# Full-row score products, late head norms and a different order of fill in a two-layer hybrid encoder

## The chip, the cores and the metric

The kernel runs on one core of a Trainium2 chip. Its time is the device time of one execution in microseconds (us). A core has a matrix engine (TensorE, PE in the profile; its weight loads are shown apart as PEld), a vector engine (VectorE, DVE), an activation engine (ScalarE, ACT), a general engine (GpSimd, POOL) and a queue engine that issues transfers (SyncE, SP). They run side by side and wait for each other through semaphores. Matrix results land in PSUM, which has eight banks of 512 fp32 columns here: four buffers called `mm`, two called `sc` (scores) and two called `tr` (transposes). All else lies in SBUF.

## The reference, cut to what matters

Batch 1, 512 tokens in a grid of 8 x 64, width 1024, two layers, fp32. Each layer does three things to x:

```python
h = rms_norm(x, norm_mix)
proj = h @ w_in                          # local q,k,v (8 heads x 64), then g_q (8), g_k (2), g_v (2)
na  = neighbourhood_attention(...)       # 8 heads, window 8 x 16, learned bias
g_q = rope(rms_norm(g_q per head, q_norm)); g_k = rope(rms_norm(g_k per head, k_norm))
gqa = softmax(g_q @ g_k.T * 64**-0.5) @ g_v       # 8 query heads over 2 key heads
x = x + concat([na, gqa]) @ w_out
q = rms_norm(x, norm_mem_q) @ w_mem_q             # 4 heads x 128
k, v = rms_norm(mem, norm_mem_kv) @ w_mem_kv      # 256 memory tokens
x = x + softmax(q @ k.T * 128**-0.5) @ v @ w_mem_o
u = conv3(rms_norm(x, norm_ffn) @ w_up) ; x = x + (silu(gate) * val) @ w_down
```

A last RMS norm follows.

## The kernel before, in words

x is held transposed, features on partitions, as eight tiles `xT` of 128 x 512. Every operand of a product is split in two: a high part in the fp32r format, made by an ACT copy, and a low part, the rest, made by a subtraction. A product is then three matmuls (`mm3`): high by high, high by low, low by high. Weights come as `raw` tiles over SP's queue, and `emit_split` (L192, L193) casts them on ACT and subtracts on POOL or DVE; the order of all weights is written out in `plan_layer`, and `get_w` hands them out in that order, splitting a few ahead.

PE and SP keep the program's order. ACT, DVE and POOL instructions are put in order by a scheduler when the program is built.

The order on PE is woven by hand. `weave` runs pipeline steps of attention units (scores, normalise, transpose, values), each a fixed number of rounds behind the other, and between them takes steps of a `Filler`, a list of generators with projection work. `NA_FILL`, `GQA_FILL` and `MEM_FILL` say how many steps of fill each round gets; `MEM_STEPS` does so for the statistics and operands of the memory in layer 0.

A layer runs through these stages. First comes local attention (`na_...`), eight units of two heads and two query blocks, with the projections of q, k, v and then of the grouped heads (`gqa_project`) as fill. `split_qk` scales a projected q or k, and makes the stacked operand: for q one tile per head with the high part in the head's 64 partitions and the low part in the other 64; for k the high part in both halves, and the low part apart. The scores of one head are therefore a 128-row matmul (q high and low by k high) and a 64-row one (q high by k low). `na_normalise` scales the exponentials by the reciprocal sums, half of them on DVE and half on POOL (`normalise`, L388).

`gqa_rope` norms and rotates the heads of one block of 128 tokens: ACT copies them out of PSUM (L684) and squares them (L686), DVE sums, multiplies by the cosine table (L690), POOL multiplies by the sine table (L695), and an inverse root is taken (L312 on DVE, L314 on POOL). One block later, through `late` and `tick`, `gqa_rope_end` adds the two products (L701) and multiplies by the root (L702).

Then four rounds of `gqa_transpose` turn the heads and build the same kind of stacked operands (L719 to L728), and sixteen units of grouped-query attention follow, with fill: memory keys, memory values, the output product of the local heads (`out_na`), and the first rows of the output product of the grouped heads (`close_rows("outg", ...)`). `fold` brings the two heads of a pair, which lie in one half of the partitions, into one tile.

`close_rows` finishes a row of x: it keeps three rows open until the last operand is there, and `Norm.close` adds x (L339), makes the next norm's operand (ACT L348, DVE L349), copies x back (ACT L341) and squares it (ACT L353, sums on POOL L364). Memory attention then projects its queries from the unnormed operand; the norm's factor, `rs`, enters as scale of the exponentials (L911, L915), so the scores need not wait for the statistics. The FFN comes last.

## Time and profile before

| what | before |
|---|---|
| time, median of 3 (lowest to highest) | 1415.34 us (1415.29 to 1416.22) |
| the profiled execution's own time | 1416.86 us |
| its span | 1415.0 us |
| mean granted clock of TensorE | 0.992 |
| matmuls | 7236 |
| transfers | 128.61 MB, mean 91 GB/s |

The span is the time between the first and the last instruction that the profiler saw; the remaining 1.86 us lie around it. Rows of the profile name an engine, a line of the kernel, the operation, the tile written and the tiles read. Almost all PE work has line L60, a helper, so it is told apart by the tiles: `mm<-xg,hi` is a projection with a normed x, `sc` are scores, `tr` transposes. Matmuls overlap in the records: the time of one from start to end is longer than the distance to the next one's start, and this distance is what it costs.

### The profile page before, as it was taken

How to read it: one execution, taken by the hardware profiler on the slowest of the kernel's cores; microseconds unless marked ns; L12 is line 12 of the kernel's file. 1: busy time of each engine (PE TensorE's matmuls, PEld its weight loads, DVE VectorE, ACT ScalarE, POOL GpSimd, SP SyncE). 2: the span in 40 equal slices, each digit the busy share in tenths (PEclk: the TensorE clock that was granted, in tenths of full speed). 3: DMA queues.
4: the chain of work that ended last, by engine and by line, in shares of the span. 5: the costliest groups of instructions: out<-in, count | busy, mean ns of one | idle time of the engine just before them, and what ended most of it. 6: DMA issues, size and time to landing. Idle time of an engine off the chain costs nothing.

```text
span 1415.0 us, 19554 instructions
## 1 busy us (share of the span) xinstructions
PE 1366.4 (97%) x7236; PEld 1152.7 (81%) x7236; DVE 932.9 (66%) x1606; ACT 720.3 (51%) x1350; POOL 700.5 (50%) x509
## 2 busy tenths in 40 slices
PE   8999799989999999999999998999899999999997
PEld 7788777877888888888888887788788888888897
DVE  5889977565588169458457898754738843871874
ACT  5776667656443234233557666766555432432441
POOL 2347755734444444544544686456164444444452
PEclk9999999999999999999999999999999999999999
DMA  6431321222333333332343223122133333333331
GB/s 211 152 97 46 91 75 31 76 74 60 90 104 90 104 110 106 97 104 84 96 147 99 83 62 118 31 61 89 31 91 101 91 105 90 101 91 106 88 91 60
DMA packets 207070, 128.61 MB, mean 91 GB/s; under 512 B 4608, under 2 KB 203520, under 8 KB 206976
## 3 DMA queue, kind: packets, MB, share of 16 engines
q1 hardware_dynamic: 206976, 127.37, 30.4%
q8 instruction: 57, 0.93, 0.3%
q14 instruction: 37, 0.30, 0.1%
HBM read 125.26 MB, written 2.10 MB: 90 GB/s over the span
## 4 chain that ended last, share of the span: by engine, by line
PE 77%; DVE 13%; ACT 5%; issue 2%; DMA 2%; POOL 1%; SPq 0%; DVEq 0%; ACTq 0%
PE mm L60 71%; PE tr L60 3%; PE sc L60 3%; DVE r L382 1%; ACT hi L192 1%; DVE t L645 1%; DMA raw<-in_w_in 1%; ACT t L603 1%; DVE t L388 1%; DVE r L548 1%; DVE sc L597 1%; DVE xg L721 1%; POOL lo L193 1%; DVE r L701 1%; DVE s L911 1%
## 5 line engine op out<-in xcount | busy, mean ns | idle before, releaser
L193 POOL TENSOR_TENSOR lo<-raw,hi 128x512 fp32r<-128x512 f32 (+2 forms) x264 | 501.1, 1909 | 522.9 <-ACT hi L192 520.8
L60 PE MATMUL mm<-xg,hi 128*128 128x512 f32 x1792 | 557.1, 392 | 4.4 <-DVE r L385 2.5
L60 PEld LDWEIGHTS mm<-xg,hi 128*128 128x128 f32 x1792 | 335.2, 189 | 74.6 <-issue 2.6
L192 ACT CAST hi<-raw 128x512 fp32r<-128x512 f32 (+2 forms) x276 | 224.5, 837 | 313.0 <-PE mm L60 257.8
L60 PE MATMUL mm<-xg,lo 128*128 128x512 f32 x896 | 350.1, 391 | 0.0
L60 PE MATMUL mm<-r,hi 128*128 128x512 f32 (+1 forms) x1160 | 338.7, 376 | 3.9 <-DVE r L385 2.3
L60 PEld LDWEIGHTS mm<-r,hi 128*128 128x128 f32 x1160 | 210.9, 190 | 43.0 <-issue 3.9
L1010 DVE SCALAR_TENSOR_TENSOR t<-t,par,t 128x7 f32<-128x7 f32 (+1 forms) x352 | 201.4, 639 | 32.0 <-ACT t L1003 31.6
L60 PE MATMUL mm<-r,lo 128*128 128x512 f32 (+1 forms) x580 | 216.8, 374 | 0.0
L60 PEld LDWEIGHTS mm<-xg,lo 128*128 128x128 f32 x896 | 168.7, 188 | 35.9 <-DVE lo L193 0.7
L60 PE MATMUL mm<-hi,xg 128*128 128x256 f32 x640 | 122.5, 286 | 4.1 <-ACT t L684 2.9
L60 PEld LDWEIGHTS mm<-r,lo 128*128 128x128 f32 x580 | 110.0, 190 | 19.3
L388 POOL TENSOR_SCALAR t<-t,s 128x512 f32<-128x512 f32 (+1 forms) x96 | 62.8, 667 | 111.7 <-DVE s L609 53.0
L995 DVE TENSOR_TENSOR t<-mm,rep 128x512 f32<-128x512 f32 x88 | 60.1, 687 | 75.5 <-PE mm L60 59.7
L60 PEld LDWEIGHTS mm<-hi,xg 128*128 128x128 f32 x640 | 101.9, 191 | 7.3 <-ACT t L684 3.9
L60 PE MATMUL mm<-r,r 128*128 128x256 f32 (+1 forms) x684 | 102.8, 299 | 3.8 <-DVE r L382 3.8
L60 PEld LDWEIGHTS mm<-r,r 128*128 128x128 f32 x684 | 88.7, 191 | 13.8 <-issue 5.9
L1012 ACT ACTIVATE t<-t 128x512 f32<-128x512 f32 x44 | 27.8, 633 | 127.1 <-DVE t L1010 127.1
L1039 DVE TENSOR_TENSOR xT<-xT,mm 128x512 f32<-128x512 f32 x32 | 22.0, 686 | 106.7 <-PE mm L60 106.7
L1016 DVE TENSOR_TENSOR r<-t,r 128x512 fp32r<-128x512 f32 x44 | 87.1, 1979 | 7.3 <-ACT r L1015 4.1
L60 PE MATMUL mm<-lo,xg 128*128 128x256 f32 x320 | 90.5, 283 | 0.0
L382 DVE TENSOR_TENSOR r<-tr,r 128x512 fp32r<-128x512 f32 x112 | 74.6, 685 | 6.8 <-ACT r L381 5.9
(129 smaller groups left out, 1652.5 us busy)
## 6 DMA issues: line engine op xcount, KB each, us to landing
raw<-in_w_up SPq DMA_DIRECT2D x88, 512.0 KB, 3.9
raw<-in_w_in SPq DMA_DIRECT2D x34, 512.0 KB, 4.1
raw<-in_w_down SPq DMA_DIRECT2D x32, 448.0 KB, 3.8
raw<-in_w_mem_kv SPq DMA_DIRECT2D x16, 512.0 KB, 3.8
raw<-in_w_down SPq DMA_DIRECT2D x16, 512.0 KB, 4.2
r<-in_bias SPq DMA_DIRECT2D x16, 384.0 KB, 4.7
raw<-in_w_out SPq DMA_DIRECT2D x8, 512.0 KB, 3.5
raw<-in_w_out SPq DMA_DIRECT2D x16, 256.0 KB, 4.2
```

The costliest lines, as they stand in the source:

```text
L60: return lambda *a, **k: self.tc.keep_in_program_order(op(*a, **k))
L192: act.copy(hi[:, k], raw[:, k])
L193: (POOL if eng[0] == "P" else DVE).tensor_sub(lo[:, k], raw[:, k], f(hi)[:, k])
L382: DVE.tensor_sub(lo, ps, f(hi))
L388: eng.tensor_scalar(e, e, sums[:, col : col + 1], 1.0, op0=ALU.mult, op1=ALU.mult)
L548: DVE.tensor_sub(v[o] if n == "q" else qk[n, p][2][r], u[r], f(v[r]))
L597: DVE.tensor_tensor_reduce(out=sc[j][:, i, :], in0=sc[j][:, i, :], in1=bias[p][j][:, WTYPE[b], :], op0=ALU.add, op1=ALU.min, scale=-1.0, s ...
L995: DVE.tensor_mul(u, us[side], ffn.rep)
L1010: DVE.scalar_tensor_tensor(cc[:, dst], u[:, src], wi, cc[:, dst], op0=ALU.mult, op1=ALU.add)
L1012: ACT.activation(cs[0], cs[0], AF.Silu)
L1016: DVE.tensor_sub(acts[j][1], cs[0], f(acts[j][0]))
L1039: DVE.tensor_add(xT[m], xT[m], pm)
```

## The change

The change has these parts, in both layers:

- Scores of both attentions: the low part of k is now stored in both halves of the partitions, so that the second score product is a full 128-row one as well. The number of matmuls stays.
- `split_qk` scales q and k in place in PSUM and splits from there; k's second copy is made on ACT.
- Local attention's weights: the half that DVE scaled is scaled on ACT.
- The grouped heads are projected in the order keys and values, first queries, second queries. The sums of squares of all blocks are gathered, and the inverse root is taken once per group. Rotated heads are added at once, from a product left in PSUM and POOL's product. k is multiplied by its root on POOL; q's root is the scale of the exponentials, with the bias multiplied by it on ACT.
- Memory keys are projected between the grouped heads' projections; memory values follow; half of the grouped heads' output product (two of four head pairs) is added to x in a generator of its own, and `close_rows` takes the other half. `outg` weights are cut in 2 x 512 columns instead of 4 x 256.
- `fold` writes each half of 256 columns directly as high and low parts.
- Memory queries are scaled by the norm's factor before they are split: the factor is spread over columns (`mq.spread()`), and the scores' maximum is used as it is.

The core of the diff:

```diff
+GQA_ORDER = [2, 0, 1]
+MEMK_AFTER = [(0,), (1, 2), (3,)]
-NA_FILL = [(2, 0, 0), (3, 0, 1), (2, 1, 1), (0, 1, 1), (1, 1, 1), (0, 2, 1), (1, 1, 1), (1, 1, 1), (1, 1, 1), (0, 3, 1)]
+NA_FILL = [(2, 0, 1), (2, 0, 1), (1, 1, 1), (1, 1, 1), (1, 1, 1), (1, 1, 1), (1, 1, 1), (1, 1, 1), (1, 1, 2), (1, 2, 1)]
-GQA_FILL = [1, 2, 1, 2, 1, 1, 1, 1, 1, 1, 1, 1, 1, 1, 1, 1, 1, 1, 0, 6]
+GQA_FILL = [1, 1, 1, 1, 1, 2, 1, 1, 1, 1, 2, 1, 1, 1, 1, 1, 1, 1, 0, 6]
-MEM_STEPS = [1, 0, 0, 1, 0, 2, 1, 0, 0, 3]
+MEM_STEPS = [1, 0, 1, 1, 1, 1, 2, 3, 0, 0]
...
     def split_qk(n, p, pm):
-            u = tmp()
             if n == "q":
-                DVE.scalar_tensor_tensor(u, pm, HD**-0.5, mix.rep, op0=ALU.mult, op1=ALU.mult)
+                DVE.scalar_tensor_tensor(pm, pm, HD**-0.5, mix.rep, op0=ALU.mult, op1=ALU.mult)
...
+            lows = rtile((2, S))
+            qk[n, p] += [lows[:, j] for j in range(2)]
+            for j, (v, r, o) in enumerate(halves):
+                for half in (r, o):
+                    DVE.tensor_sub(lows[half, j], pm[r], f(v[r]))
+                ACT.copy(v[o], pm[r])
...
                 for j in range(2):
-                    PE.matmul(sc[j][:, i, :], qst[j][:, qs], kst[j][:, ks], start=True, stop=False)
-                for j in range(2):
-                    r = slice(64 * j, 64 * j + 64)
-                    PE.matmul(sc[j][:, i, :], qst[j][r, qs], kst[2][r, ks], start=False, stop=True)
+                    for part in range(2):
+                        PE.matmul(sc[j][:, i, :], qst[j][:, qs], kst[2 * part + j][:, ks], start=part == 0, stop=part == 1)
...
-                    normalise(es[j][:, i, :], sums, 2 * j + i, POOL if i else DVE)
+                    if i:
+                        normalise(es[j][:, i, :], sums, 2 * j + i, POOL)
+                    else:
+                        ACT.activation(es[j][:, i, :], es[j][:, i, :], AF.Copy, scale=sums[:, 2 * j + i : 2 * j + i + 1])
...
+            ACT.activation(x, pv, AF.Copy, scale=r)
+            ACT.activation(tq, pv, AF.Square, scale=r)
+            DVE.scalar_tensor_tensor(pv, pv, r, gtab[0][:, 2 * qk, b, :].unsqueeze(1).to_broadcast([P, nh, HD]),
+                                     op0=ALU.mult, op1=ALU.mult)
+            DVE.tensor_reduce(hs, tq, axis=AX.X, op=ALU.add)
...
-            hr = rsqrt(hs, nh, 1.0 / HD)
-            late.append(lambda: gqa_rope_end(t1, t2[:, :nh], hr, nh))
-        def gqa_rope_end(t1, t2, hr, nh):
-            DVE.tensor_add(t1, t1, t2)
-            DVE.tensor_mul(t1, t1, hr.unsqueeze(2).to_broadcast([P, nh, HD]))
+            DVE.tensor_add(roped[b][:, g:8:2, :] if g < 2 else roped[b][:, 8:10, :], pv, t2)
...
-                        DVE.tensor_sub(gq[0][r, 5, bs], tr[r, 0], f(g[r, 4, bs]))
-                    for g, r, o in halves:
-                        DVE.tensor_copy(g[o, 4, bs], g[r, 4, bs])
+                        for half in (r, o):
+                            DVE.tensor_sub(g[half, 5, bs], tr[r, 0], f(g[r, 4, bs]))
+                        ACT.copy(g[o, 4, bs], tr[r, 0])
...
+                c, r = slice(j, j + 1), hq[j][:, 4 * b + i : 4 * b + i + 1]
+                DVE.tensor_reduce(nmx[:, c], sc[j], axis=AX.X, op=ALU.max, negate=True)
+                ACT.activation(nb[:, c], nmx[:, c], AF.Copy, scale=r)
-                ACT.activation(e, sc[j], AF.Exp, bias=nmx[:, j : j + 1], accum_out=sums[:, j : j + 1])
+                ACT.activation(e, sc[j], AF.Exp, bias=nb[:, c], scale=r, accum_out=sums[:, c])
...
+        def out_gqa():
+            for m in range(KC):
+                if m % 4 == 0:
+                    w = get_w(("outg", 0, m // 4))
+                pm = ps_mm()
+                gemm_T(pm, w, parts[4:6], range(2), 0, 1, slice(P * (m % 4), P * (m % 4) + P))
+                DVE.tensor_add(xT[m], xT[m], pm)
+                yield
...
-        fill = Filler(*([project_first(), *units[3:]] if l == 0 else units), gqa_project())
+        gqa = [gen for g, heads in zip(GQA_ORDER, MEMK_AFTER) for gen in (gqa_project(g), memory_keys(heads))]
+        fill = Filler(*([project_first(), *units[3:]] if l == 0 else units), *gqa)
...
-        fill = Filler(memory_keys(), memory_values(0), out_na(), memory_values(1), close_rows("outg", PartsView(parts, 4), nn))
+        fill = Filler(memory_values(0), memory_values(1), out_na(), out_gqa(), close_rows("outg", 1, PartsView(parts, 6), 2, nn))
...
+        def mem_query(h, pm):
+            DVE.scalar_tensor_tensor(pm, pm, 128.0**-0.5, mq.rep, op0=ALU.mult, op1=ALU.mult)
+            mqs[h] = rpair()
+            split_psum(*mqs[h], pm)
...
-            nmx, sums, nb = small(2), small(2), small(2)
+            nmx, sums = small(2), small(2)
             DVE.tensor_reduce(nmx, sc, axis=AX.X, op=ALU.max, negate=True)
-            DVE.tensor_mul(nb, nmx, rs[:, 2 * bp : 2 * bp + 2])
...
         mq.stat()
         fill.step(2)
-        DVE.tensor_scalar_mul(rs, mq.rstd, 128.0**-0.5)
+        mq.spread()
+        for h, pm in unscaled:
+            mem_query(h, pm)
+        unscaled = None
+        fill.step(1)
```

More of the change, by code (lines that the diff above doesn't have):

```diff
@@ L396, in fold @@
         for j, r in enumerate(rows):
-            DVE.tensor_add(o32[r, cs], po[0:64, j], th[r, j])
+            DVE.tensor_add(o32[r], po[0:64, j], th[r, j])
+        ACT.copy(out[0][:, cs], o32)
+        POOL.tensor_sub(out[1][:, cs], o32, f(out[0][:, cs]))
     def split_out(o32):
@@ L541, in split_qk @@
             for v, r, o in halves:
[L542 to L544 removed]
+                ACT.copy(v[r], pm[r])
+            if n == "q":
                 for v, r, o in halves:
[L546 to L548 removed]
+                    DVE.tensor_sub(v[o], pm[r], f(v[r]))
+                return
+            lows = rtile((2, S))
[4 more added lines that the diff above has]
+                ACT.copy(v[o], pm[r])
         vblk = [None, None]
@@ L680, in gqa_rope @@
+        def gqa_rope(g, b, pm, hs):
             nh = 4 if g < 2 else 2
```

166 lines of the change are left out of this document (78 added, 88 removed).

## The prediction

> **What bounds the kernel now.** I read the page's busy shares, then the windows of busy time by stage, then the groups of instructions inside the first attention stage, then the timeline around the edited places.
>
> ```profile
> PE 1366.4 (97%) x7236; PEld 1152.7 (81%) x7236; DVE 932.9 (66%) x1606; ACT 720.3 (51%) x1350; POOL 700.5 (50%) x509
> ...
> 50.00:180.00 130.00, 116.28 (x813) 104.52 (x813) 114.77 (x254) 89.62 (x216) 83.41 (x90) 0.99 0.28 86
> 180.00:265.00 85.00, 84.41 (x514) 68.05 (x515) 56.91 (x110) 58.24 (x135) 47.38 (x53) 1.00 0.21 57
> 265.00:292.00 27.00, 26.64 (x122) 21.91 (x121) 11.71 (x18) 17.94 (x30) 17.15 (x10) 1.00 0.26 78
> 292.00:330.00 38.00, 33.74 (x174) 27.35 (x174) 27.37 (x57) 20.20 (x51) 10.51 (x5) 0.96 0.18 56
> 740.00:870.00 130.00, 121.95 (x866) 110.95 (x864) 109.74 (x252) 89.06 (x213) 82.81 (x89) 0.99 0.31 95
> 981.00:1020.00 39.00, 34.73 (x181) 28.39 (x182) 27.38 (x57) 20.80 (x51) 10.52 (x5) 0.96 0.18 54
> 400.00:425.00 25.00, 25.00 (x112) 20.71 (x111) 21.44 (x30) 11.40 (x15) 10.74 (x5) 1.00 0.35 101
> ```
>
> The first column after the stretch is its length, then busy time of PE, PEld, DVE, ACT, POOL. PE is busy 97% of the span, so time comes from two places only: what PE is kept busy with, and about 48 us of holes (1415.0 less 1366.4). The holes lie where the change works. Local attention with its projections (50 to 180, and 740 to 870 in layer 1) leaves PE idle 13.7 and 8.05 us, and there DVE is the fullest of the others, at 88% and 84%. Memory attention (292 to 330, 981 to 1020) leaves 4.26 and 4.27 us. The grouped-query stage between (180 to 265) has no hole: 84.41 of 85. In the FFN a 512-column matmul takes a slot of 25.00/112 = 0.223 us.
>
> **Score products on all rows.** What a 64-row product costs is read from when the next instruction starts, since a busy PE here includes its drains.
>
> ```profile
> 740.21 1.46 PE L60 MATMUL sc<-r,r 128*128 128x256 f32 x8
> 741.60 0.38 PE L60 MATMUL mm<-hi,xg 128*128 128x256 f32 x1
> ...
> 741.94 0.40 PE L60 MATMUL mm<-hi,xg 128*128 128x256 f32 x2
> ...
> 742.30 0.40 PE L60 MATMUL mm<-hi,xg 128*128 128x256 f32 x2
> ...
> 206.02 1.14 PE L60 MATMUL sc<-xg 128*128 128x512 f32 x3
> 206.67 0.50 PE L60 MATMUL sc<-xg,xg 64*128 64x512 f32 x1
> 207.10 0.39 PE L60 MATMUL mm<-r,r 128*128 128x256 f32 x1
> ```
>
> A local unit's eight score matmuls hold PE from 740.21 to 741.60, 1.39 us. Full 256-column matmuls come three per 0.36 us (741.94 to 742.30), 0.12 us each, so eight full ones need 0.96: 0.43 saved. A grouped-query unit holds PE from 206.02 to 207.10, 1.08 us; its last two products start together at 206.67. Four full 512-column slots are 4 x 0.223 = 0.89: 0.19 saved. With 8 local and 16 grouped-query units per layer, two layers: 16 x 0.43 + 32 x 0.19 = **-13.0**. PE is the bound there, so it counts in full; its ends are 0 and -13.
>
> The Trainium skill (TensorEngine Tiling (Array Packing), Theoretical Speedup) speaks against this edit: contraction of up to 64 rows is to be tiled for up to twice the speed. The 206.67 row agrees that the two halves run side by side. The same page of the Trainium skill (Key Properties) says that changing the mode drains the array; the 0.65 us from 206.02 to 206.67 for two full products, against 0.446 for two slots, fits that.
>
> **Work taken from DVE in local attention (both layers).**
>
> ```profile
> L388 DVE TENSOR_SCALAR t<-t,s 128x256 f32<-128x256 f32 x16 | 8.7, 588 | 0.4
> L548 DVE TENSOR_TENSOR r<-t,r 64x512 fp32r<-64x512 f32 x8 | 9.7, 1215 | 0.7 <-ACT r L542 0.5
> L546 DVE CAST r<-r 64x512 fp32r<-64x512 f32 x4 | 3.2, 812 | 0.5 <-ACT r L542 0.4
> L728 DVE CAST xg<-xg 64x128 fp32r<-64x128 f32 x8 | 5.7, 717 | 0.2
> L721 DVE TENSOR_TENSOR xg<-tr,xg 64x512 fp32r<-64x512 f32 x8 | 5.5, 689 | 0.1
> L726 DVE TENSOR_TENSOR xg<-tr,xg 64x128 fp32r<-64x128 f32 x8 | 2.3, 289 | 0.1
> L702 DVE TENSOR_TENSOR r<-r,s 128x256 f32<-128x256 f32 x8 | 4.9, 610 | 0.0
> L312 DVE TENSOR_SCALAR s<-s 128x2 f32<-128x2 f32 x4 | 2.7, 684 | 0.1
> L312 DVE TENSOR_SCALAR s<-s 128x4 f32<-128x4 f32 x8 | 2.3, 291 | 0.1
> ...
> L686 ACT ACTIVATE t<-t 128x256 f32<-128x256 f32 x8 | 3.3, 418 | 0.2
> L719 ACT CAST xg<-tr 64x512 fp32r<-64x512 f32 x8 | 4.7, 582 | 7.4 <-PE tr L60 7.4
> L724 ACT CAST xg<-tr 64x128 fp32r<-64x128 f32 x8 | 2.1, 261 | 0.4 <-PE tr L60 0.2
> ...
> 301.49 0.16 DVE L911 TENSOR_TENSOR s<-s,s 128x2 f32<-128x2 f32 x1
> ...
> 303.96 2.40 POOL L193 TENSOR_TENSOR lo<-raw,hi 128x1024 fp32r<-128x1024 f32 x1 [6.06 <-ACT hi L192]
> ...
> 304.43 1.95 DVE L911 TENSOR_TENSOR s<-s,s 128x2 f32<-128x2 f32 x1
> ```
>
> These are groups of 50 to 180 alone. The local weights' scaling leaves DVE: -8.7. The low parts of q and k are now subtracted out of PSUM; L721 is that form at 0.689 against 1.215: 8 x 0.526 = -4.2, and k's four casts (3.2) become four more such subtractions (2.8): -0.4. The key casts of the grouped stage become subtractions like L726: 5.7 - 8 x 0.289 = -3.4. The head-norm multiplication goes: -4.9. Twelve L312 become three: 5.0 x 9/12 = -3.7. Together -25, so DVE falls from 114.8 to about 90 of 130. ACT takes 16 scalings at L686's 0.418 (6.7), four second copies of k at L719's 0.582 (2.3), eight small ones at L724's 0.261 (2.1): 89.6 + 11 = 101 of 130, 78%, the new fullest. POOL loses most of its power operations and gets four small products for k.
>
> The last three rows show why PSUM sources matter: a two-element product of two SBUF tiles took 0.16 us, and 1.95 us when it began 0.47 us into a POOL subtraction that ended at 306.36. The Trainium skill (SBUF — State Buffer, Who interferes with whom) has a rule for it: a VectorE instruction with two SBUF inputs waits for a GpSimd one that reads SBUF. The trace agrees, with the 1.95.
>
> How much of the 21.8 us of PE holes (13.7 + 8.05) closes? Between the layers 4 points of DVE share go with 5.7 us of holes; at 78% on ACT the line would leave none, but chains from exponential to sum to scaling to transposition remain, and layer 0 also waits for memory statistics. I leave 9: **-12.8**, ends 0 (ACT takes DVE's place) and -21.8.
>
> **Memory keys and half the output rows as fill.** No matmul is saved. The keys, 4 x 24 x 0.12 = 11.5 us of PE per layer, move into the stage with the holes; that is how the -12.8 can be had, and is not counted again. Their weight DMAs move on SP's queue ahead of memory-value weights, of equal bytes; DMA share there is 0.28. The output half moves into 180 to 265, where PE is full, so it gains nothing; its eight extra additions per layer lie beside PE, DVE having 56.91 of 85. But they leave the closing rows with less cover.
>
> ```profile
> L348 ACT ACTIVATE xg<-mm,par 128x512 fp32r<-128x512 f32 x40 | 26.8, 697 | 2.2 <-DVE mm L339 2.2
> L353 ACT ACTIVATE t<-mm 128x512 f32<-128x512 f32 x40 | 24.9, 623 | 0.0
> L341 ACT COPY xT<-mm 128x512 f32<-128x512 f32 x40 | 23.9, 598 | 9.0 <-DVE xg L349 9.0
> L192 ACT CAST hi<-raw 128x1024 fp32r<-128x1024 f32 x120 | 126.0, 1050 | 237.1 <-PE mm L60 207.8 <-issue 17.2 <-DMA raw<-in_w_up 10.3
> L747 ACT ACTIVATION_READ_ACCUMULATOR t<-sc,s 128x1 f32 x64 | 12.5, 196 | 0.0
> ...
> 294.51 1.02 POOL L314 TENSOR_TENSOR s<-s,mhalf 128x4 f32<-128x4 f32 x1
> 294.68 0.88 PE L60 MATMUL sc<-r,r 128*128 128x256 f32 x6
> ...
> 153.22 0.37 ACT L684 ACTIVATE t<-mm,s 128x128 f32<-128x128 f32 x1 [0.35 <-POOL s L314]
> ...
> 156.24 0.78 POOL L695 TENSOR_TENSOR r<-t,r 128x64 f32<-128x64 f32 x2
> ```
>
> Closing one row takes three ACT operations, 0.697 + 0.623 + 0.598 = 1.92 us. So far PE spent 12 x 0.223 = 2.68 per row, now 6 x 0.223 = 1.34. After the last part is ready PE has 3 x 3 + 5 x 6 = 39 closing matmuls and 36 of the first two memory queries, 75 x 0.223 = 16.7 us, before it needs row 7; ACT needs 8 x 1.92 plus about three weight casts at 1.05, 18.5. So PE waits some 2 us per layer: **+4**, ends 0 (casts done early) and +10 (ACT's order and four mm buffers make it 5 per layer).
>
> **Memory queries scaled ahead of the scores.** In layer 0 the scores began at 294.68 while the reciprocal root was only being formed (294.51 + 1.02 = 295.53). Now PE waits for it to spread it over columns, at a cost of about 0.85 us. Then come an ACT copy (0.582, as L719), a DVE product (0.689, as L721), ACT high part (0.582) and DVE low part (0.689): 2.5 us and some hand-over, less one more step of fill, 6 x 0.223 = 1.34. About 2 us more of waiting; behind it on PE stand the third query's matmuls and all scores. Against it the two-element product, L911, leaves the chain of every unit, and with it POOL's block of up to 1.95. That can return at most the holes of 4.26 and 4.27; I take 3 per layer, about what is added: **0**, ends -5 and +6.
>
> **Scaled exponentials.** Each grouped-query unit gets two tiny ACT operations, bounded by the 128x1 row at 0.196: 0.4 x 16 = 6.3 us per layer beside 58.24 of 85 busy; the cover is PE's own 4 us per unit. Were it gone, 0.4 x 32 = +12.5. I take 0.
>
> **Sum.** -13.0 - 12.8 + 4 + 0 = -22. The profiled execution took 1416.86 us (span 1415.0 and 1.86 around it); it lies 1.5 above the median, 1415.34. From the former 1395, from the median **1393.5**, which is what I forecast.
>
> **The rivals.**
> (a) ACT takes DVE's place: the holes of local attention stay. For it: 78% on ACT, with weight casts in the same queue, and layer 1 had 8 us of holes at 84%. Against: ACT writes no operand that POOL blocks. Time: 1415.3 - 13 + 4 = 1406.
> (b) Slower: PSUM is held until POOL has finished. A projection block's buffer was read for the last time by ACT or DVE directly; now it is overwritten in place and added after POOL's rotary products. In the quoted case the ACT copy started at 153.22 and POOL's products ended at 157.02, 3.8 us on. A block lasts 24 x 0.12 = 2.9 us, and with four mm buffers shared with two value products the hold may last some 5.8 us. It decides if POOL's queue adds 2 us more, which a weight subtraction or two do. At 1.5 us over, on 12 blocks in two layers, +36: 1393.5 + 36 = 1429. Against: POOL is at 83.41 of 130, and loses power operations.
> (c) The waits around the halves are not theirs and stay, while the slot that two halves share is lost: 32 x 0.223 + 16 x 0.24 = +11 and no -13, so 1415.3 - 12.8 + 4 + 11 = 1417.5. Against: the start times above. This is how the tiling rule of the Trainium skill (TensorEngine Tiling (Array Packing), Theoretical Speedup) would have it.
> (d) The change does nothing on balance: close, query wait and tiny operations at their costs (+10, +6, +12.5) eat the 26 of gain: 1417.
>
> **How the numbers follow.** Forecast 0.62, its own range 1381 to 1402; (a) 0.17; (b) 0.13; (c) 0.03; (d) 0.05. A measurement of this kernel can tell 0.2% (2.8 us) from no change. Faster: forecast and (a), and a little of (d), 0.80. Same: (c) and part of (d), 0.05. Slower: (b) and the rest, 0.15. The range reaches from the forecast with all holes closed and no closing loss, and 3 us gained in the memory stage, 1415.3 - 13 - 21.8 - 3 = 1377.5, to the edge of (a) with the closing at +10 and half the tiny operations, 1418; (b) and a small rest are left out.
>
> **What would show it.** Right: no 64*128 group; the units' scores about 0.96 and 0.9 us from start to next start; DVE near 90 and ACT near 100 in the first stage, PE's holes there halved; a hole of some 2 us in the closing rows, with ACT as the releaser, and one before the first memory score. Wrong: PE waiting on mm buffers for POOL-fed additions (L701's successor), ACT above 95% in local attention, or score units as long as before.

## The result, and the profile after

The kernel with the change takes 1421.82 us (median of 5 runs, 1420.32 to 1423.62) against 1415.34: a ratio of 1.0044, 95% interval 1.0029 to 1.0058. It is slower, by 6.5 us, where 22 less were forecast, and it lies above the upper end of the range, 1418. The profiled execution took 1420.8 us, span 1418.9.

The page's busy shares of the kernel after:

```profile
PE 1360.9 (96%) x7252; PEld 1165.1 (82%) x7252; DVE 879.1 (62%) x1538; ACT 768.9 (54%) x1488; POOL 683.1 (48%) x507
```

DVE gave up 54 us and ACT took 49, as meant. PE is busy 5.5 us less, and the span is 3.9 longer: PE's holes grew from 48.6 to 58.0 us. Where they lie is read from the windows, cut at the first score of each attention, so that each stretch spans the same stages in both kernels. The local stretch reaches to the first grouped score, so it also holds the four rounds of `gqa_transpose` and the fill between them. First before: local attention and grouped units of layer 0, then of layer 1 (length, then busy time of PE, PEld, DVE, ACT, POOL, granted clock, DMA share, GB/s).

```profile
40.40:179.17 138.77, 123.83 (x870) 111.26 (x869) 123.39 (x269) 94.52 (x226) 83.38 (x91) 0.99 0.29 90
179.17:246.19 67.02, 66.10 (x382) 50.73 (x382) 49.14 (x95) 47.24 (x112) 35.72 (x42) 1.00 0.18 48
...
740.21:868.45 128.24, 121.01 (x862) 110.37 (x861) 108.14 (x248) 88.99 (x213) 81.71 (x89) 0.99 0.31 96
868.45:935.79 67.34, 66.24 (x382) 50.75 (x383) 49.22 (x95) 47.35 (x112) 35.75 (x42) 1.00 0.18 48
```

The same four stretches after:

```profile
44.46:191.53 147.07, 131.93 (x948) 124.91 (x947) 95.60 (x233) 110.91 (x265) 84.99 (x93) 0.95 0.30 95
191.53:258.95 67.42, 63.66 (x366) 52.29 (x365) 49.24 (x92) 56.53 (x142) 32.74 (x41) 1.00 0.15 40
...
744.52:877.26 132.74, 125.44 (x940) 119.48 (x939) 85.26 (x219) 106.05 (x252) 84.40 (x92) 0.99 0.35 108
877.26:945.53 68.27, 63.89 (x367) 52.38 (x365) 49.25 (x92) 56.64 (x142) 32.72 (x41) 1.00 0.15 40
```

A hole is length less PE's busy time. The local stretch holds 78 more matmuls per layer and 23 to 28 us less of DVE, but its holes are as large as they were: 14.94 and 7.23 before, 15.14 and 7.30 after, though no other engine is above 80% there. The grouped units had 0.92 and 1.10 us of holes and have 3.76 and 4.38. In layer 0's local attention the clock fell to 0.95.

The 78 matmuls are not the memory keys. The 96 of these (`mm<-r,hi` and `mm<-r,lo` of 256 columns) lie in this stretch in both kernels: before among the transpositions, from 157.0 us on, and after among the projections, from 126.2 us on. New in the stretch is what took their old place: 72 matmuls of the memory values and 6 of the first row of `out_na`. These are the larger group of the keys (64 in both kernels) and that of the values, in layer 0's stretch of before, and then the values after:

```profile
L60 PE MATMUL mm<-r,hi 128*128 128x256 f32 x64 | 12.0, 288 | 2.3 <-DVE r L385 2.3
...
L60 PE MATMUL mm<-hi,r 128*128 128x256 f32 x16 | 3.1, 287 | 0.0
```

```profile
L64 PE MATMUL mm<-hi,r 128*128 128x256 f32 x64 | 13.8, 308 | 0.0
```

The holes are not the old ones either. This is what PE waited for in the local stretch (us, layer 0 and layer 1, added up from the view of waits of each stretch):

| PE waited for | before | after |
|---|---|---|
| low parts from `split_psum` (DVE L382, L385; after L387, L390) | 6.8, 1.9 | 1.7, 0.5 |
| the rotary copy out of PSUM (ACT L684) | 1.8, 1.1 | none |
| low parts of transposed heads (DVE L721, L726; after L734) | 3.7, 3.4 | 0.5, none |
| second copies of k (ACT L741, L559 after) | none | 8.7, 4.8 |
| the memory's factor and its sums, layer 0 | 0.9 | 3.9 |
| other | 0.9, none | 0.3, 2.0 |

So the waits that were there before did shrink, and new ones, made by the change itself, took their room.

The rest of the stages, cut in the same way (worked out from such windows):

| stage | length before, after (us) | holes before, after (us) |
|---|---|---|
| start to the first local score | 40.40, 44.46 | 4.11, 5.60 |
| last grouped score to first memory score, layer 0 | 48.48, 46.05 | 0.36, 3.65 |
| the same, layer 1 | 48.48, 47.14 | 0.36, 3.39 |
| memory attention to the FFN, layer 0 | 73.72, 68.35 | 4.82, 2.52 |
| the same, layer 1 | 73.37, 68.44 | 4.54, 2.49 |

Who ended PE's waits after, from the view of waits (us in total, times, longest):

```profile
PE tr L64 <- ACT xg L741: 9.6, 4, 2.9
PE sc L64 <- ACT t L760: 6.6, 11, 1.6
PE mm L64 <- ACT t L358: 4.9, 5, 2.1
PE mm L64 <- ACT r L559: 3.6, 1, 3.6
```

Four places, all on ACT: L741 and L559 are the second copies of k, L760 is the scaled exponential, L358 the square in the closing rows. The first is seen in the timeline, in the last transposition of a key group:

```profile
188.69 0.48 PE L64 MATMUL tr<-ident,r 128*128 128x128 f32 x1 [2.94 <-ACT xg L741]
...
189.21 0.53 ACT L737 CAST xg<-tr 64x128 fp32r<-64x128 f32 x2 [0.57 <-PE tr L64]
...
189.78 0.58 DVE L740 TENSOR_TENSOR xg<-tr,xg 64x128 fp32r<-64x128 f32 x2 [1.04 <-ACT xg L737]
...
190.39 0.26 ACT L741 CAST xg<-tr 64x128 fp32r<-64x128 f32 x1 [0.65 <-DVE xg L740]
...
190.68 0.60 DVE L740 TENSOR_TENSOR xg<-tr,xg 64x128 fp32r<-64x128 f32 x2 [0.33 <-ACT xg L741]
...
191.32 0.26 ACT L741 CAST xg<-tr 64x128 fp32r<-64x128 f32 x1 [0.67 <-DVE xg L740]
```

All of ACT's and DVE's operations here read one tile `tr` in PSUM, and none writes it. Still they run strictly in turn, as the code has them: ACT's high part, DVE's two subtractions, ACT's copy, DVE's for the other half, ACT's copy. Each engine starts 0.03 to 0.04 us after the other one ends. The numbers in brackets are the idle time of an engine before its row, which here is mostly the other one's work. The buffer is held until the last, from 189.21 to 191.58. The Trainium skill (PSUM — Partial Sum Buffer, PSUM bank collisions raise a hardware error) says why they are ordered: two engines may not touch the same bank and partitions at once, reads included. The trace agrees: in the rows above ACT and DVE never overlap.

The second place, the first grouped unit:

```profile
192.19 1.29 DVE L757 TENSOR_REDUCE s<-sc 128x1 f32<-128x512 f32 x2 [0.91 <-PE sc L64]
...
192.92 0.29 ACT L758 ACTIVATE s<-s,s 128x1 f32<-128x1 f32 x1 [1.34 <-DVE s L757]
...
193.25 0.78 ACT L760 ACTIVATE t<-sc,s,s 128x512 f32<-128x512 f32 x1
...
193.92 0.19 ACT L760 ACTIVATION_READ_ACCUMULATOR t<-sc,s,s 128x1 f32 x1
194.02 0.28 ACT L758 ACTIVATE s<-s,s 128x1 f32<-128x1 f32 x1
...
194.17 0.74 PE L64 MATMUL sc<-xg 128*128 128x512 f32 x2 [0.15 <-ACT t L760]
```

Between the maximum and the release of the score buffer stand the tiny product and a longer exponential. Their prices, from the groups: the first row is of before (plain), the next two of after.

```profile
L747 ACT ACTIVATE t<-sc,s 128x512 f32<-128x512 f32 x64 | 43.8, 687 | 29.7 <-DVE s L745 29.5
```

```profile
L760 ACT ACTIVATE t<-sc,s,s 128x512 f32<-128x512 f32 x64 | 49.9, 780 | 2.6
L758 ACT ACTIVATE s<-s,s 128x1 f32<-128x1 f32 x64 | 18.8, 294 | 14.1 <-DVE s L757 13.5
```

Before, ACT idled 29.7 us in front of these exponentials; after, 2.6 there and 14.1 ahead of the tiny product. Each costs 0.780 + 0.294 where it cost 0.687. The price could have been read before the change. Local attention's exponentials (L603) have the same shape as those of the memory stage (L915), and only the latter take their scale from a tile; after the change the memory stage lacks it too (two rows of before, then one of after):

```profile
L603 ACT ACTIVATE t<-sc,s 128x256 f32<-128x256 f32 x64 | 29.6, 473 | 39.6 <-DVE s L597 39.5
L915 ACT ACTIVATE t<-sc,s,s 128x256 f32<-128x256 f32 x32 | 17.8, 562 | 21.2 <-DVE s L911 21.2
```

```profile
L943 ACT ACTIVATE t<-sc,s 128x256 f32<-128x256 f32 x32 | 15.0, 476 | 11.6 <-DVE s L940 11.6
```

The score products themselves, after. The first two rows are a grouped unit, the other two a local one:

```profile
216.07 1.17 PE L64 MATMUL sc<-xg 128*128 128x512 f32 x4
...
217.08 1.11 PE L64 MATMUL mm<-r,r 128*128 128x256 f32 x8
...
753.99 1.12 PE L64 MATMUL sc<-r,r 128*128 128x256 f32 x8
...
754.94 0.63 PE L64 MATMUL mm<-xg,hi 128*128 128x512 f32 x2
```

The grouped unit takes 1.01 us, where 0.89 was forecast (before 1.08). The local one takes 0.95, forecast 0.96 (before 1.39).

### The profile page after: what moved, and what is told of

Read it like the earlier page. It is cut to its first block, busy times and chain, and to the rows that moved or that the text cites. A ratio compares the mean times of both kernels' runs of the same rounds, so it can differ in the third digit from the quotient of the medians.

```text
span 1418.9 us, 19659 instructions
## 1 busy us (share of the span) xinstructions
PE 1360.9 (96%) x7252; PEld 1165.1 (82%) x7252; DVE 879.1 (62%) x1538; ACT 768.9 (54%) x1488; POOL 683.1 (48%) x507
## 4 chain that ended last, share of the span: by engine, by line
PE 81%; ACT 7%; DVE 4%; POOL 3%; issue 2%; DMA 1%; SPq 0%; DVEq 0%; ACTq 0%; POOLq 0%
PE mm L64 75%; PE tr L64 4%; PE sc L64 3%; POOL lo L197 2%; ACT hi L196 2%; ACT t L612 1%; DVE r L387 1%; ACT t L760 1%; DMA r<-in_w_in 1%; DVE sc L606 1%; POOL s L319 0%; DMA raw<-in_w_in 0%; DVE r L558 0%; ACT r L548 0%; DVE s L757 0%
## 5 line engine op out<-in xcount | busy, mean ns | idle before, releaser
L197 POOL TENSOR_TENSOR lo<-raw,hi 128x512 fp32r<-128x512 f32 (+2 forms) x264 | 495.6, 1888 | 533.5 <-ACT hi L196 512.5
L64 PE MATMUL mm<-hi,xg 128*128 128x256 f32 x640 | 125.9, 292 | 8.1 <-ACT r L559 3.6
L64 PEld LDWEIGHTS mm<-hi,xg 128*128 128x128 f32 x640 | 105.6, 198 | 9.3 <-ACT r L559 3.8
L393 POOL TENSOR_SCALAR t<-t,s 128x512 f32<-128x512 f32 (+1 forms) x96 | 58.5, 622 | 104.0 <-DVE s L766 58.2
L64 PE MATMUL mm<-r,r 128*128 128x256 f32 (+1 forms) x684 | 98.2, 292 | 1.2 <-DVE r L387 1.2
L1043 ACT ACTIVATE t<-t 128x512 f32<-128x512 f32 x44 | 27.8, 633 | 126.6 <-DVE t L1041 126.6
L387 DVE TENSOR_TENSOR r<-tr,r 128x512 fp32r<-128x512 f32 x112 | 74.5, 684 | 13.0 <-ACT r L386 12.6
```

The source lines that it names most:

```text
L64: return lambda *a, **k: self.tc.keep_in_program_order(op(*a, **k))
L197: (POOL if eng[0] == "P" else DVE).tensor_sub(lo[:, k], raw[:, k], f(hi)[:, k])
L387: DVE.tensor_sub(lo, ps, f(hi))
L393: eng.tensor_scalar(e, e, sums[:, col : col + 1], 1.0, op0=ALU.mult, op1=ALU.mult)
L1043: ACT.activation(cs[0], cs[0], AF.Silu)
```

## The experiments

Times are medians, ratios are to the kernel before in runs beside them.

**Three suspected costs, each by itself.** The theory was that the tax of shared PSUM tiles, the scaled exponentials and the thinner cover of the closing rows ate the gain; a further question was whether the score rows are a gain at all.

`rows_only`, the kernel before with full-row second score products alone, in both attentions (the cut shows the local one). DVE makes the doubled low parts, which adds subtractions to it:

```diff
-                DVE.tensor_sub(v[o] if n == "q" else qk[n, p][2][r], u[r], f(v[r]))
+                for to in [v[o]] if n == "q" else [lows[r, j], lows[o, j]]:
+                    DVE.tensor_sub(to, u[r], f(v[r]))
...
-                    PE.matmul(sc[j][:, i, :], qst[j][:, qs], kst[j][:, ks], start=True, stop=False)
-                for j in range(2):
-                    r = slice(64 * j, 64 * j + 64)
-                    PE.matmul(sc[j][:, i, :], qst[j][r, qs], kst[2][r, ks], start=False, stop=True)
+                    for part in range(2):
+                        PE.matmul(sc[j][:, i, :], qst[j][:, qs], kst[2 * part + j][:, ks], start=part == 0, stop=part == 1)
```

> The kernel before with one part of the change: both score products on all 128 rows, the low part of k stored in both halves by two more DVE subtractions per k and per key transposition. Theory (the 64-row products cost PE their drains, 0.43 us a local unit and 0.19 us a grouped-query unit): 13.0 us off PE, less about 5 us for 16 subtractions of about 1 us more on DVE where DVE is fullest, so 1402 to 1410 us against 1415.3. Rival (the two halves side by side are worth more than the drain): 1415 to 1426.

1416.4, ratio 1.0011 [1.0002, 1.0021]: no gain at all, so the theory missed. Three of its windows, cut as above:

```profile
38.92:181.57 142.65, 122.40 (x870) 113.95 (x868) 127.05 (x283) 94.64 (x226) 83.13 (x91) 0.96 0.28 88
181.57:246.57 65.00, 64.02 (x384) 54.73 (x384) 49.12 (x98) 47.66 (x112) 35.82 (x42) 1.00 0.18 50
739.66:869.62 129.96, 117.45 (x863) 110.41 (x861) 111.42 (x261) 88.49 (x213) 81.86 (x89) 0.99 0.30 94
```

The grouped units got 2.0 and 2.3 us shorter. In local attention PE's work fell by 1.4 and 3.6, but its holes rose from 14.94 and 7.23 to 20.25 and 12.51: work taken from PE there turned into waiting. DVE was 3.7 and 3.3 us fuller, at 89% of layer 0's stretch. Whether the added subtractions made the holes, or PE's shorter work exposed waits that were there, this run does not tell apart.

`own_bank`, the change with q and k scaled into an SBUF tile and split from there, and the second key copy read from SBUF:

```diff
+            src, pm = pm, tmp()
-                DVE.scalar_tensor_tensor(pm, pm, HD**-0.5, mix.rep, op0=ALU.mult, op1=ALU.mult)
+                DVE.scalar_tensor_tensor(pm, src, HD**-0.5, mix.rep, op0=ALU.mult, op1=ALU.mult)
...
-                        ACT.copy(g[o, 4, bs], tr[r, 0])
+                        ACT.copy(g[o, 4, bs], f(g[r, 4, bs]))
```

> The changed kernel, except that q and k are scaled into an SBUF tile and split from there, and that the second copy of the grouped keys is read from SBUF. Theory A (ACT and DVE may not use one PSUM tile at the same time, so the splits run in turn and hold mm and tr buffers): the PE waits for the second key copies (4.8 us in each layer), for k's second copy (3.6) and for the subtraction at the start (2.3) go, 15.5 us, with some half-clock windows: 1402 to 1409 us against 1421.8. Rival B (ACT is full and has taken DVE's place): ACT has the same operations and DVE longer ones, so 1420 to 1426.

1415.09, ratio 1.0000 [0.9991, 1.0009]: 6.7 us less than the change, a smaller step than expected, in the expected direction.

```profile
0.00:38.96 38.96, 35.98 (x180) 30.47 (x181) 24.18 (x36) 24.63 (x42) 10.79 (x14) 0.96 0.75 233
...
185.69:256.42 70.73, 65.95 (x366) 53.48 (x367) 51.03 (x97) 57.89 (x144) 35.55 (x44) 0.98 0.17 45
742.03:870.98 128.95, 124.75 (x940) 118.23 (x938) 85.78 (x215) 104.43 (x250) 83.33 (x90) 1.00 0.34 108
```

The start came down from 44.46 to 38.96, layer 1's local attention from 132.74 to 128.95; the waits of 9.6 for L741 and 3.6 for L559 are gone. Layer 0's local attention did not get shorter (146.73 after 147.07): there PE's wait for `split_psum`'s low parts of the values (L390) rose from 0.5 to 6.7 us in their place. The grouped units gave back 3.3 and 2.5: the cost of the exponentials was still there, and the clock fell to 0.98. The turns of the two readers and the longer hold of the buffer went together here, so their shares are not known.

`plain_exp`, the change without the scale and the tiny product; q's head norm is left out of the computation.

```diff
-                ACT.activation(nb[:, c], nmx[:, c], AF.Copy, scale=r)
-                ACT.activation(e, sc[j], AF.Exp, bias=nb[:, c], scale=r, accum_out=sums[:, c])
+                ACT.activation(e, sc[j], AF.Exp, bias=nmx[:, c], accum_out=sums[:, c])
```

> The changed kernel without q's head norm in the grouped-query exponentials: no scale operand and no multiplied bias (this leaves out that factor of the computation). Theory C (the scaled exponential, 0.779 against 0.688 us, and the tiny ACT operation before it lengthen the hold of the two score buffers): the new holes in the grouped-query units, 2.8 and 3.3 us, go: 1414 to 1417 us against 1421.8, ACT's exponential back at 0.69. Rival (the units are not held by the score buffers): 1420 to 1422.

1412.27, ratio 0.9975 [0.9965, 0.9986]: 9.6 less than the change, more than the 5 to 8 expected.

```profile
189.95:254.34 64.39, 63.79 (x367) 53.90 (x366) 48.35 (x92) 46.80 (x112) 33.39 (x42) 0.98 0.16 42
875.31:938.67 63.36, 62.76 (x367) 52.86 (x365) 48.25 (x92) 46.85 (x112) 33.39 (x42) 1.00 0.16 43
```

The grouped units' holes fall to 0.60 in both layers, and the stage by 3.0 and 4.9 us: there most of the cost lies. How it divides between the scale and the tiny product was not tried.

`close_all`, the change with all four head pairs in the closing rows, as before, and no generator for the other half. The `outg` weights are cut in four again, and `GQA_FILL` is set to the shorter list of fill.

```diff
-        fill = Filler(memory_values(0), memory_values(1), out_na(), out_gqa(), close_rows("outg", 1, PartsView(parts, 6), 2, nn))
+        fill = Filler(memory_values(0), memory_values(1), out_na(), close_rows("outg", 1, PartsView(parts, 4), 4, nn))
```

> The changed kernel with all four head pairs of the grouped output product in the closing rows, as before, and no half of it as fill. Theory D (the closing rows have lost the PE work that covered ACT): the new holes there, 3.3 and 3.0 us with a wait for the square on ACT of 2.1 us, go: 1414 to 1417 us against 1421.8. Rival (the holes there come from elsewhere, or the fill is missed among the units): 1420 to 1428.

1427.63, ratio 1.0086 [1.0073, 1.0100]: 5.8 more than the change.

```profile
191.63:259.32 67.69, 62.31 (x354) 51.01 (x353) 47.97 (x91) 56.38 (x143) 32.46 (x41) 0.98 0.13 32
259.32:308.26 48.94, 45.48 (x231) 37.45 (x229) 19.90 (x34) 28.17 (x53) 28.25 (x21) 1.00 0.21 65
```

By the total this is a miss, and by the trace the theory held. The wait for the square on ACT, at the same matmul of the closing rows, in three kernels: before, after, and `close_all`.

```profile
270.47 0.73 PE L60 MATMUL mm<-r,hi 128*128 128x512 f32 x2 [0.36 <-ACT t L353]
```

```profile
281.64 0.73 PE L64 MATMUL mm<-r,hi 128*128 128x512 f32 x2 [2.07 <-ACT t L358]
```

```profile
279.92 0.74 PE L64 MATMUL mm<-r,hi 128*128 128x512 f32 x2 [0.36 <-ACT t L357]
```

With the cover of before, the wait is that of before, in layer 1 too (0.36 after 2.07). So thin cover is what opened it. The stretch's hole stayed near its size (3.46 after 3.65) because other waits came: 0.81 and 0.89 us of the last units' transpositions, which had lost their fill. Twelve matmuls fewer did not shorten the grouped units either (67.69 after 67.42); they only made their holes larger. In these two kernels, half of the product is better placed as fill, in spite of the 2 us.

**A version without the two taxes, and its parts undone.** `mended` is `own_bank` with plain exponentials, and q multiplied by its root on DVE once the group is done.

```diff
             hq[g] = rsqrt(sums, NB * nh, 1.0 / HD)
+            if g < 2:
+                for b in range(NB):
+                    q = roped[b][:, g:8:2, :]
+                    DVE.tensor_mul(q, q, hq[g][:, 4 * b : 4 * b + 4].unsqueeze(2).to_broadcast([P, 4, HD]))
```

> The changed kernel with both costs taken off: q and k split from an SBUF tile and the second key copy read from SBUF (as in own_bank), and q's root multiplied into the rotated heads on DVE, so that the exponential has no scale operand and no multiplied bias. Theory (two separate taxes, 6.7 and 9.6 us, on a change whose other parts gain): 1421.8 - 6.7 - 9.6 + about 3 for eight DVE products of 0.45 per layer, so 1406 to 1411 us against 1415.1. Rival (the two share one cause, so that they do not add up): 1412 to 1416.

1414.86, ratio 1.0006 [0.9996, 1.0015]: missed, and inside the rival's range, though `free_exp` below speaks against the rival's reason. The grouped units are short (65.5 and 65.8), but local attention grew to 153.04 and 133.37, with a new wait of PE, once in each layer, for the products with the root (the waits, whole run):

```profile
PE tr L64 <- DVE r L694: 6.2, 2, 3.1
```

The root of a whole group and four products behind it now stand in front of the first transposition. The products took 1.26 us each, where 0.45 had been expected. It is still a base for undoing parts.

`m_dve_scale`: DVE scales its half of the local weights again.

```diff
-                        ACT.activation(es[j][:, i, :], es[j][:, i, :], AF.Copy, scale=sums[:, 2 * j + i : 2 * j + i + 1])
+                        normalise(es[j][:, i, :], sums, 2 * j + i, DVE)
```

> The mended kernel with the local weights' scaling back on DVE. Theory (local attention is held by chains and no longer by DVE's load): within 2 us of the mended kernel, either way. Rival (the prediction's reason: DVE's load makes the holes, 8.7 us of it per layer): 4 to 8 us slower than the mended kernel.

1422.8, ratio 1.0057 [1.0043, 1.0071]: 7.9 more than `mended`. Relieving DVE pays, nearly all of it in layer 0: in the profiled runs its local stretch is 157.13 us after 153.04 and the stretch before it 40.61 after 39.01, while layer 1's local stretch is 133.90 after 133.37.

`m_late_keys`: the memory keys are projected behind local attention's and the grouped heads' projections again. The lists of fill follow, and so does the order of the weights (not shown).

```diff
-NA_FILL = [(2, 0, 1), (2, 0, 1), (1, 1, 1), (1, 1, 1), (1, 1, 1), (1, 1, 1), (1, 1, 1), (1, 1, 1), (1, 1, 2), (1, 2, 1)]
-GQA_FILL = [1, 1, 1, 1, 1, 2, 1, 1, 1, 1, 2, 1, 1, 1, 1, 1, 1, 1, 0, 6]
+NA_FILL = [(2, 0, 1), (2, 0, 1), (1, 1, 1), (1, 1, 1), (1, 1, 1), (1, 1, 1), (1, 1, 1), (1, 1, 1), (0, 1, 1), (0, 1, 1)]
+GQA_FILL = [2, 2, 2, 2, 1, 2, 1, 1, 1, 1, 2, 1, 1, 1, 1, 1, 1, 1, 0, 6]
...
-        gqa = [gen for g, heads in zip(GQA_ORDER, MEMK_AFTER) for gen in (gqa_project(g), memory_keys(heads))]
+        gqa = [gqa_project(g) for g in GQA_ORDER]
...
-        fill = Filler(memory_values(0), memory_values(1), out_na(), ...
+        fill = Filler(memory_keys(range(4)), memory_values(0), memory_values(1), out_na(), ...
```

> The mended kernel with the memory keys back behind local attention, as fill among the key transpositions and the grouped-query units. Theory (the holes of local attention are waits of chains that fill does not shorten): within 3 us of the mended kernel. Rival (the keys fill holes there, as the prediction had it): 6 to 12 us slower, since their 11.5 us of PE per layer then come on top of a full stage.

1426.4, ratio 1.0087 [1.0073, 1.0101]: 11.5 more than `mended`. Local attention, layers 0 and 1:

```profile
41.28:189.09 147.81, 124.40 (x870) 116.29 (x869) 105.39 (x237) 106.76 (x254) 77.46 (x86) 0.93 0.26 85
748.60:879.72 131.12, 116.69 (x863) 110.34 (x861) 91.37 (x218) 99.99 (x240) 76.07 (x84) 0.97 0.29 94
```

Its holes are 23.41 and 14.43, against 17.95 and 8.54 in `mended`: 11.4 us more, which is the whole difference. The number falls into the rival's range, but nearly all of it is one wait, the same that was new in `mended` (there 3.1 us at most):

```profile
PE tr L64 <- DVE r L694: 16.2, 2, 8.1
```

With less fill between the last projection and the first transposition, PE stands there for 8.1 us in each layer, until the group's root and its products are done. So 10.0 of the 11.4 us are lost cover for a chain that the change itself does not have. What the keys' place among the projections is worth in the change, no run shows.

`m_rs`: memory attention as before the change, with the reciprocal root in the exponentials' scale and bias.

```diff
-MEM_FILL = [1, 1, 1, 2, 1, 0, 0, 2, 0, 1, 2]
+MEM_FILL = [2, 1, 1, 2, 1, 0, 0, 2, 0, 1, 2]
...
-                ACT.activation(e[:, i, :], sc[:, i, :], AF.Exp, bias=nmx[:, i : i + 1], accum_out=sums[:, i : i + 1])
+                b = 2 * bp + i
+                ACT.activation(e[:, i, :], sc[:, i, :], AF.Exp, bias=nb[:, i : i + 1], scale=rs[:, b : b + 1],
+                               accum_out=sums[:, i : i + 1])
...
-        mq.spread()
-        for h, pm in unscaled:
-            mem_query(h, pm)
-        unscaled = None
-        fill.step(1)
+        DVE.tensor_scalar_mul(rs, mq.rstd, 128.0**-0.5)
```

> The mended kernel with memory attention as before the change: the norm's factor as scale of the exponentials, no spreading. The prediction held the two ways equal (0, ends -5 and +6): within 2 us of the mended kernel. Rival 1 (a scale operand costs the exponential, 0.564 against 0.476 us here, and L911 is blocked by POOL): 3 to 8 us slower. Rival 2 (the wait for the spread factor is the larger): 2 to 6 us faster.

1414.47, ratio 1.0003 [0.9994, 1.0012], 0.4 from `mended`: no difference.

**Both taxes off, and where q's root may go.** `free_exp` is `own_bank` with the plain exponentials of `plain_exp`; q's head norm is left out.

> The kernel of own_bank without q's head norm in the exponentials (this leaves that factor out of the computation). Theory (two taxes of 6.7 and 9.6 us, each by itself, and mended lost the second gain again to its DVE products at the end of the projections): 1421.8 - 6.7 - 9.6 = 1405.5, so 1403 to 1409 us. Rival (the two overlap): 1411 to 1415.

1403.41, ratio 0.9920 [0.9906, 0.9934]: 18.4 less than the change, where the two taxes by themselves sum to 6.7 + 9.6 = 16.3. They add up, and 11.5 us of gain against the kernel before appear.

`block_roots` is `free_exp` with q's norm again: its root is taken block by block, and the product comes one block later on DVE.

```diff
                 gqa_rope(g, b, pm, sums[:, b * nh : b * nh + nh])
+                if g < 2:
+                    tick()
+                    q, hr = roped[b][:, g:8:2, :], rsqrt(sums[:, b * nh : b * nh + nh], nh, 1.0 / HD)
+                    late.append(lambda q=q, hr=hr: DVE.tensor_mul(q, q, hr.unsqueeze(2).to_broadcast([P, 4, HD])))
```

> The mended kernel, with q's root taken and multiplied in block by block, one block late, instead of once for a group behind its last block. Theory (mended's new hole of 3.0 us per layer in front of the key transpositions is the group's root, 3.1 us on POOL, and four products behind it; only the last block's root is exposed now): 4 to 8 us off the mended kernel's 1414.9, so 1407 to 1411 us. Rival (more small operations on DVE and POOL cost as much as the hole): 1413 to 1418.

1409.9, ratio 0.9961 [0.9948, 0.9974]: faster than both kernels, 5.0 under `mended`. PE's wait for the group's root is gone. The 6.5 us above `free_exp` are the price of q's norm in this place.

`b_pairs` is `block_roots` with 64-row second score products, in both attentions (the cut shows the local one). The doubled low parts are still made, so only PE's work differs.

```diff
-                    for part in range(2):
-                        PE.matmul(sc[j][:, i, :], qst[j][:, qs], kst[2 * part + j][:, ks], start=part == 0, stop=part == 1)
+                    PE.matmul(sc[j][:, i, :], qst[j][:, qs], kst[j][:, ks], start=True, stop=False)
+                for j in range(2):
+                    r = slice(64 * j, 64 * j + 64)
+                    PE.matmul(sc[j][:, i, :], qst[j][r, qs], kst[2 + j][r, ks], start=False, stop=True)
```

> The kernel of block_roots with the second score products on 64 rows again, all else alike. Theory (a pair's drain costs 0.43 us per local and 0.19 us per grouped-query unit, where PE is the bound): 8 to 15 us slower than block_roots. Rival (the score products are hidden behind other waits): within 3 us of it.

1420.34, ratio 1.0037 [1.0023, 1.0051]: 10.4 more than `block_roots`. Grouped units of layer 0, first of `block_roots`, then of `b_pairs`:

```profile
188.37:252.72 64.35, 62.30 (x366) 52.88 (x366) 50.11 (x97) 47.95 (x114) 35.83 (x44) 1.00 0.18 50
```

```profile
190.63:257.28 66.65, 65.65 (x365) 49.13 (x365) 50.52 (x97) 48.08 (x114) 35.59 (x44) 1.00 0.17 48
```

The stage is 2.30 us longer for 16 units, 0.14 each, and 2.24 us in layer 1. Local attention is 1.45 and 3.75 us longer, while its holes are 1.1 and 0.2 us smaller. So here the full rows count nearly in full, although the stretch has holes of 15 and 5 us.

`b_mem_later` is `block_roots` with one list changed, the steps of the memory statistics between the units of layer 0's local attention.

```diff
-MEM_STEPS = [1, 0, 1, 1, 1, 1, 2, 3, 0, 0]
+MEM_STEPS = [1, 0, 0, 1, 1, 2, 2, 2, 0, 0]
```

> The kernel of block_roots with the memory statistics of layer 0 one round later (MEM_STEPS 1, 0, 0, 1, 1, 2, 2, 2). Theory (layer 0's local attention is held by PE waiting for the spread of the memory's factor, 2.9 us, and for v's split behind the two reductions of 2 us on DVE, 4.3 us, and by the half clock after them): 3 to 8 us faster than block_roots, all of it in layer 0. Rival (these waits only move): within 2 us of it.

1407.95, ratio 0.9950 [0.9937, 0.9963]: 2.0 under `block_roots`, short of the 3 to 8 expected and no more than the rival allows, and the intervals of the two overlap. Layer 0's local attention, first of `block_roots`, then of `b_mem_later`:

```profile
39.39:188.37 148.98, 133.97 (x948) 125.10 (x946) 110.33 (x249) 112.41 (x266) 89.70 (x99) 0.95 0.30 95
```

```profile
40.21:186.67 146.46, 130.69 (x949) 121.96 (x947) 110.42 (x248) 110.97 (x264) 88.22 (x98) 0.98 0.30 96
```

The holes did not shrink (15.01 and 15.77 us); the clock rose from 0.95 to 0.98, and PE did the same work in 3.3 us less. Whether the list does that in general, or the holes fell kindly here, one profile of each cannot tell.

## Why the prediction was wrong, point by point

- **Local attention, -12.8, holes from 21.8 to 9.** This step failed. The holes are 22.4 after. Its reason was sound as far as it went: the old waits shrank from 12.3 and 6.4 us to 2.2 and 0.5, and DVE's relief is worth 7.9 by its main part in `mended`. What the prediction had no term for are the waits that the edit brings in the same place: the second copies of k (the third point below) hold PE for 8.7 and 4.8 us, and the memory's factor for 3 us more in layer 0. Taking the copies out of PSUM helped layer 1 (`own_bank`, 4.20 us of holes) and left layer 0 at 14.09.
- **The keys, "how it can be had".** This rests on a misreading. The window of 50 to 180 us, from which the prediction read its holes, held the keys already, among the transpositions. What came into the stage is the memory values. `m_late_keys` does not show what the move is worth.
- **Low parts out of PSUM, counted at -4.2, -0.4 and -3.4.** The price of the operation was right: 0.689 us, and DVE fell by 27.8 and 22.9 us in the two local stretches against a forecast of 25. What the prediction left out is that ACT then reads the same tile in turn with DVE, and that the buffer is held until the last of them: `own_bank`, without that, is 6.7 us faster. Rival (b), which named held PSUM buffers, had the right resource with the wrong holder: ACT and DVE in turn, and not POOL.
- **Scaled exponentials, 0.** This failed: 9.6 us. The tiny operation was bounded by the 128x1 accumulator row at 0.196 and takes 0.294. The scale operand's 0.09 us was not counted, though two rows of before showed it (L915 at 0.562, L603 at 0.473). Above all, the cover was named as PE's 4 us per unit, when PE waits on two score buffers: with 2 x (0.294 + 0.093) us added inside their hold, ACT's idle time ahead of them fell from 29.7 to 2.6 + 14.1, and PE came to wait for them. The "+12.5 if the cover is gone" was nearer to the truth.
- **Score rows, -13.0, "PE is the bound there, so it counts in full".** In `block_roots` they are worth 10.4, so the step was right in kind and too large. The grouped unit was mis-sized: four full 512-column products took 1.00 to 1.01 us and not four slots, 0.89, which makes the saving 0.07 us per unit and not 0.19. In `rows_only` they were worth nothing; there DVE was near 90% and had more to do.
- **Closing rows, +4, thin cover.** Right, in size and in reason. The waits for the square grew by 2.0 and 1.7 us, and with full cover they went.
- **Memory queries, 0.** Right by `m_rs`, 0.4 us. The wait that was foretold before the first memory score is there, 0.69 us.
- **Rival (a), ACT in DVE's place.** Half of it came true. The holes stayed, and most of the new waits are for ACT; but ACT is not full, with 111 and 106 of 147 and 133 us in local attention, 75% and 80%. PE waits for single copies behind DVE. Rival (c), the tiling rule of the Trainium skill (TensorEngine Tiling (Array Packing), Theoretical Speedup), would have made 64-row pairs the faster form; `b_pairs`, 10.4 us slower, speaks against it here. Rival (d), 1417 by its text and 1418 by its sum, is nearest in time, but by luck: of its three costs at their full size, only that of the tiny operations came.
- **The clock** was in none of the steps. Half of the time that TensorE spent at half clock is 11.9 us before and 18.1 after, in the profiled runs. So up to 6 us of the change's loss came through the clock, as far as PE had work in these windows.

The costs of the shared PSUM tiles and of the exponentials together are 18.4 us (`free_exp`), of the 28.3 by which the forecast was off. `free_exp` is still 9.9 us above the forecast. The score rows, 2.6 short, and its local holes, 13.1 and 4.0 us where 9 in all were forecast, come to about that much; this is a sum over different kernels, and not a measurement. Who makes those holes was not tried, beyond the one list of the memory statistics.

## What to carry to other kernels

Holes that keep their size need not be the same holes. Before counting a wait as closed, list the waits that the edit itself brings to the same buffers and the same place, and afterwards compare who released them, and not only how long they are. When a PSUM tile gets a second reader on another engine, count the turns and the hold of its buffer, and not the operations alone. Price a "free" scale or a tiny operation inside the loop between two buffers by the idle time that its engine has there. And when a part is undone on another base, look which wait made the difference: it may be one that only that base has.

## What the runs showed of the hardware that had not been expected

- **Short holes halve the clock for a fixed window.** In the clock records of all runs, TensorE drops to half speed for windows of 3.413 us, which within a run start on one fixed grid of 3.413 us. Cutting the fourteen traces (before, after, twelve experiments) on this grid, from 20 to 1350 us: after a window in which PE was busy under 40%, the next was at half clock in 61 of 61 cases; at 40 to 50% in 16 of 22; at 50 to 60% in 7 of 42; above that in 7 of 5344. So a hole of some 2 us that falls within one window costs up to another 1.7 us of PE's work. Layer 0's local attention lost one such window before and four after (1.7 and 6.8 us). The Trainium skill (TensorE: Matmul & The Clock Gate, Part 1: The HAM clock gate) gives the free-running window of 3413 ns and the half rate, and the traces agree; it has the drop come after an idle window, and here windows that were busy up to half did it.
- **A scale given as a column of a tile costs ACT 0.09 us**: 0.780 against 0.687 us for an exponential of 128x512, 0.562 against 0.473 to 0.476 for 128x256. One element per partition, scaled in the same way, takes 0.294 us.
- **Two engines that only read a PSUM tile still took turns**, 0.03 to 0.04 us apart in the rows above, so that the tile was held for the sum of their operations, 2.37 us. That the order was needed for the result, no run here shows.
- **64-row products in pairs, between full ones, are not the faster form**: 1.39 against 0.95 us for a local unit's eight products, 1.07 against 1.00 for a grouped unit's four (`b_pairs` and `block_roots`, units in which PE did not wait).
